# Weight parts made one step apart with four pairs of buffers, expert sums accumulated in token order, and a shorter index lookup in the routing

## The chip, the cores and the metric

The kernel runs on one core of a Trainium2 chip, as one program with one launch. The metric is the device time of that launch in microseconds (us). The median of three runs of the kernel before is 1644.19 us (1643.83 to 1645.55).

The engines are named as the profile names them: PE multiplies matrices, and PEld is its weight load. DVE, ACT and POOL work on vectors. SP issues the transfers (DMA) of the weights.

## The reference

Two transformer blocks on 256 tokens of 1024 numbers, all in fp32. What matters here:

```python
# block 1: mLSTM and window attention -> w_out; cross attention -> w_xo; then the experts:
qh = (xb @ w_pq).reshape(T, P_HEADS, 2, P_KEY_DIM)             # 8 heads, two halves
s1, s2 = scores of both halves against 128 sub keys each
v1, i1 = lax.top_k(s1, 16);  v2, i2 = lax.top_k(s2, 16)
cand_s = v1[..., :, None] + v2[..., None, :]                   # 16 x 16 candidates
cand_i = i1[..., :, None] * 128 + i2[..., None, :]
top_s, pos = lax.top_k(cand_s, 16)
eidx = take_along_axis(cand_i, pos);  g = softmax(top_s)
a = gelu(einsum('thkd,td->thk', expert_down[eidx], xb))
out = einsum('thk,thkd->td', g * a, expert_up[eidx])           # 16384 experts
# block 2: rms norms of h (g_final, norm_mix), then w_in_2 (GLA and MoBA), w_branch, w_out_2, MLP, gate
```

## The kernel before

**Activations lie transposed.** `hT`, `XH` and `XL` hold 8 blocks of 128 features by 256 tokens. An fp32 product is made of three matmuls on rounded parts: the activation is `XH + XL`, the weight is `hi + lo`, and `mm3` (lines 322 to 325) adds hi·XH, hi·XL and lo·XH. One *unit* takes one weight tile of 128 x 1024. In the transposed form (`unit_T`, line 327) that is 24 matmuls of 256 columns, with the weight as the loaded operand. In the token form (`unit_N`, line 349; lines 362 to 364) it is 12 matmuls of 512 columns, with the activation loaded and the weight streaming.

**All weights come as one stream** (`Stream`, line 86), in the order of `ORDER`. `load` issues the DMA of a raw tile on SP's queue. `cut_upto` makes the two parts right after one another: `hi` is a cast, on ACT (lines 119 to 122), and `lo = raw - hi` is on DVE or POOL (line 123). `PLAN` says where: "AV" is ACT then DVE, "AG" is ACT then POOL, from the named tile on. `take` hands out one pair, after it has cut up to two tiles ahead. There are four raw tiles and three pairs of parts.

**Side work is threaded through the units** (`Chains`, line 137). Norms, attention and routing are generators. Each finished unit calls `tick`, which runs one step of every live chain, and `yield n` waits n units (`PAUSES` adds to it). A chain's step is thus queued on each engine behind the unit's evacuation. While the chain named by `gate` lives, finished units keep their PSUM bank, and five banks exist.

**The places that matter.** After the eight units `xo` of the cross attention, each evacuation adds to `hT` and makes `XH`, `XL` and a sum of squares (`add_and_prep`, line 376). Sixteen units `pq` follow, with the norm's chain `norm_chain` (line 308). Then come 128 units `down` (one per 128 experts). While these run, `routing` (line 861) does the top-k work on DVE for each of the two token blocks: sixteen `top16` of 128 scores, two in a step, then eight steps with the 16 x 16 sums and a `top16` of 256, then the softmax. The index lookup (lines 889 to 903) runs twice for each block: it compares 2048 numbers with 0 to 15, multiplies by the index, and reduces, in fp32. PE transposes what came out. After that `gating` scatters the gates, four tokens in each unit.

The stage UP (lines 970 to 995) multiplies the 128 expert tiles by their coefficients: `coef` makes both parts of 256 coefficients per tile, and `up` uses the weight as the loaded operand, 24 matmuls of 256 columns in a tile. Its sums come out transposed and are added to `hT` bank by bank. Block 2 then begins with the units `bk` of `SECOND`, which are in token form.

## Time and profile before

| | |
|---|---|
| median of the runs | 1644.19 us |
| the profiled execution | 1648.56 us, of which the span is 1646.8 us |
| PE busy | 1572.9 us, 96% of the span |
| DVE, ACT, POOL busy | 73%, 49%, 24% of the span |
| granted PE clock, mean | 0.981 of 2.4 GHz |
| `down` with the routing beside it | 300 to 505 us |
| `down` with the gating beside it | 505 to 750 us |
| UP | 753 to 1121 us |

A matmul of 256 columns is recorded as some 0.28 us long, but the next one starts 0.12 us after it: they overlap, so a full PE shows as busy and the pace has to be read from the starts. What PE waits for is told by the idle time before an instruction and by what ended it.

### The profile page before, as it was taken

What the parts mean: (1) busy time and instruction counts of PE and PEld (TensorE: products, weight loads), DVE (VectorE), ACT (ScalarE), POOL (GpSimd) and SP (SyncE); (2) the same over time, 40 slices, a digit from 0 to 9 for tenths busy, and PEclk for the clock granted to TensorE, in tenths of its full rate; (3) what the DMA queues carried; (4) which work ended last, traced back from release to release, by engine and by line L of the source; (5) the groups of instructions that cost most, each with busy time, mean ns of one, the idle gap of its engine ahead of it and who ended that gap; (6) DMA issues with size and microseconds to landing.
All of it is one profiled execution on the core that took longest, in us unless ns stands there. A gap on an engine that the chain in (4) does not pass through costs nothing.

```text
span 1646.8 us, 30594 instructions
## 1 busy us (share of the span) xinstructions
PE 1572.9 (96%) x12338; PEld 1515.7 (92%) x12338; DVE 1207.7 (73%) x2073; ACT 798.9 (49%) x1336; POOL 392.0 (24%) x223
## 2 busy tenths in 40 slices
PE   9889989989879999999999999999899999899998
PEld 8788989988879999999999999998698899899998
DVE  6967653788978899976666666668885566777556
ACT  7555443543334555544444444445464643444444
POOL 3210004435530000003444444421030100087000
PEclk9999999999989999999999999999999999999999
DMA  7334444334334444445665555665445345455653
GB/s 263 103 103 156 139 145 154 131 131 162 128 123 158 156 154 154 154 168 178 183 185 184 180 180 184 186 186 166 152 143 164 119 163 179 159 175 190 201 180 128
DMA packets 75726, 265.52 MB, mean 161 GB/s; under 512 B 8368, under 2 KB 11952, under 8 KB 75584
## 3 DMA queue, kind: packets, MB, share of 16 engines
q1 hardware_dynamic: 74848, 262.31, 48.7%
q8 instruction: 96, 1.57, 0.4%
q10 hardware_dynamic: 736, 1.27, 0.2%
q14 instruction: 46, 0.38, 0.1%
HBM read 262.49 MB, written 1.05 MB: 160 GB/s over the span
## 4 chain that ended last, share of the span: by engine, by line
PE 63%; DVE 6%; ACT 1%; issue 1%; POOL 0%; DVEq 0%; POOLq 0%; ACTq 0%
PE mm L323 11%; PE mm L325 11%; PE mm L324 10%; PE at L987 6%; PE at L988 6%; PE at L989 6%; DVE lo L123 2%; PE mm L989 2%; PE mm L988 2%; PE mm L987 2%; PE at L941 2%; PE mm L363 2%; PE mm L362 2%; PE mm L364 2%; ACT hi L122 1%
## 5 line engine op out<-in xcount | busy, mean ns | idle before, releaser
L122 ACT CAST hi<-raw 128x1024 fp32r<-128x1024 f32 (+1 forms) x495 | 515.6, 1044 | 301.0 <-issue 104.9
L123 DVE TENSOR_TENSOR lo<-raw,hi 128x1024 fp32r<-128x1024 f32 (+1 forms) x376 | 469.9, 1252 | 167.1 <-ACT hi L122 164.0
L123 POOL TENSOR_TENSOR lo<-raw,hi 128x1024 fp32r<-128x1024 f32 x119 | 296.2, 2489 | 843.5 <-ACT hi L122 708.4
L325 PE MATMUL mm<-XH,lo 128*128 128x256 f32 x1608 | 464.3, 289 | 32.2 <-DVE lo L123 31.5
L323 PE MATMUL mm<-XH,hi 128*128 128x256 f32 x1608 | 470.9, 293 | 4.8 <-DVE hT L378 4.3
L324 PE MATMUL mm<-XL,hi 128*128 128x256 f32 x1608 | 461.7, 287 | 0.0
L325 PEld LDWEIGHTS mm<-XH,lo 128*128 128x128 f32 x1608 | 315.6, 196 | 35.9 <-DVE lo L123 34.8
L323 PEld LDWEIGHTS mm<-XH,hi 128*128 128x128 f32 x1608 | 315.9, 196 | 6.6 <-issue 5.1
L324 PEld LDWEIGHTS mm<-XL,hi 128*128 128x128 f32 x1608 | 315.9, 196 | 0.2
L975 DVE SCALAR_TENSOR_TENSOR ring<-cb,ring 128x256 fp32r<-128x256 f32 x128 | 173.0, 1353 | 94.1 <-ACT ring L974 94.1
L987 PE MATMUL at<-ring,hi 128*128 128x256 f32 x768 | 217.4, 283 | 1.0 <-DVE cb L961 1.0
L988 PE MATMUL at<-ring,hi 128*128 128x256 f32 x768 | 217.4, 283 | 0.0
L989 PE MATMUL at<-ring,lo 128*128 128x256 f32 x768 | 217.4, 283 | 0.0
L987 PEld LDWEIGHTS at<-ring,hi 128*128 128x128 f32 x768 | 147.4, 192 | 1.2 <-ACT ring L974 1.2
L988 PEld LDWEIGHTS at<-ring,hi 128*128 128x128 f32 x768 | 147.4, 192 | 0.1
L989 PEld LDWEIGHTS at<-ring,lo 128*128 128x128 f32 x768 | 147.5, 192 | 0.0
L958 ACT ACTIVATE cb<-mm 128x256 f32<-128x256 f32 (+32 forms) x117 | 38.2, 326 | 171.7 <-PE mm L325 171.7
L363 PE MATMUL mm<-lo,XH 128*128 128x512 f32 (+1 forms) x208 | 82.0, 394 | 4.8 <-DVE lo L123 4.7
L362 PE MATMUL mm<-hi,XH 128*128 128x512 f32 (+1 forms) x208 | 84.1, 404 | 1.0 <-ACT kn L1336 1.0
L364 PE MATMUL mm<-hi,XL 128*128 128x512 f32 (+1 forms) x208 | 81.6, 392 | 0.8 <-DVE XL L411 0.8
L325 PE MATMUL mm<-MH,lo 128*128 128x256 f32 x256 | 72.5, 283 | 2.0 <-POOL lo L123 1.2
L988 PE MATMUL mm<-ring,hi 128*128 128x256 f32 x256 | 72.5, 283 | 0.0
(460 smaller groups left out, 2932.0 us busy)
## 6 DMA issues: line engine op xcount, KB each, us to landing
raw<-in_wst SPq DMA_DIRECT2D x237, 512.0 KB, 3.3
raw<-in_dwn SPq DMA_DIRECT2D x128, 512.0 KB, 3.3
raw<-in_upw SPq DMA_DIRECT2D x128, 512.0 KB, 4.1
hT<-in_xT SPq DMA_DIRECT2D x4, 256.0 KB, 5.4
memt<-in_memT SPq DMA_DIRECT2D x1, 1024.0 KB, 6.0
out<-hT SPq DMA_DIRECT2D x7, 128.0 KB, 1.7
rowt<-in_rows ACTq DMA_DIRECT2D x1, 640.0 KB, 6.0
raw<-in_wst SPq DMA_DIRECT2D x2, 256.0 KB, 3.9
```

What stands on the lines that cost most here:

```text
L122: self.nc.scalar.copy(hi[:, o], raw[:, o])
L123: (self.nc.vector if second == "V" else self.nc.gpsimd).tensor_tensor(lo[:, o], raw[:, o], hi[:, o], op=OP.subtract)
L323: T.matmul(ps, lhsT=wh, rhs=xh, start=start, stop=False)
L324: T.matmul(ps, lhsT=wh, rhs=xl, start=False, stop=False)
L325: T.matmul(ps, lhsT=wl, rhs=xh, start=False, stop=stop)
L362: T.matmul(pss[tb], lhsT=xh, rhs=h, start=kd == 0, stop=False)
L363: T.matmul(pss[tb], lhsT=xh, rhs=l, start=False, stop=False)
L364: T.matmul(pss[tb], lhsT=xl, rhs=h, start=False, stop=kd == 7)
L975: V.scalar_tensor_tensor(lo, cb[:, j], 1.0 / GATE, hi, op0=OP.mult, op1=OP.subtract)
L987: T.matmul(o, lhsT=wh, rhs=ch, start=j == 0 and n % 2 == 0, stop=False)
L988: T.matmul(o, lhsT=wh, rhs=cl, start=False, stop=False)
L989: T.matmul(o, lhsT=wl, rhs=ch, start=False, stop=j == 127 and n % 2 == 1)
```

## The change

1. **The second part is made one step behind the first.** `cut_upto` first makes the `lo` of tiles whose `hi` was cut a step earlier, then the new `hi`. `take` cuts one tile further ahead (4 in place of 3), so at a unit `hi` stands three tiles ahead and `lo` two, as it did. Four pairs of parts and five raw tiles are kept.
2. **`PLAN`.** POOL makes the second parts of tiles xo2 to down19 and down28 to down44 (59 tiles; before, two in three of pq2 to down51). DVE makes those of down20 to down27 and of down45 to down127.
3. **UP in token form.** The coefficients are the loaded operand and 512 columns of the weight stream: 12 matmuls in a tile, into four PSUM banks. At the end the sums are copied to SBUF (two copies on ACT, two on DVE), turned by 16 transposes on PE, and only then added to `hT`; the second half of this is a chain that starts in the first tick of `bk`.
4. **The lookup** works on fp16, with a shape in which neighbouring numbers lie in pairs: 2048 compared, 2048 multiplied, and four additions that halve the 16 rows (1024, 512, 256 and 128) in place of the reduction. Each lookup step waits five units in place of four.
5. **Norms.** `norm_chain` waits two units before its last matmuls in place of one (three for the memory's; the first norm keeps one). `along` and `gla` wait one unit longer.
6. The coefficients of UP share their buffers with the gating's tiles.

```diff
+PLAN = {"mv0": ("AV",), "xo2": ("AG",), "down20": ("AV",), "down28": ("AG",), "down45": ("AV",),
+        "upw0": ("AV", "AG"), "upw122": ("AV",), "up3": ("AV", "AG"), "up31": ("AV",)}
...
-    def cut_upto(self, upto):
+    def cut_upto(self, upto, lag=1):
+        self.second_upto(upto - lag)
         while self.cut < min(upto, len(self.order)):
...
+    def second_upto(self, upto):
+        while self.second < min(upto, self.cut):
+            c = self.second
+            hi, eng = self.parts[c]
+            lo = self.split.tile([128, 1024], FR, tag="lo", name="lo")
+            raw = self.raws.pop(c)
+            for o in self.halves(c):
+                (self.nc.vector if eng == "V" else self.nc.gpsimd).tensor_tensor(lo[:, o], raw[:, o], hi[:, o],
+                                                                                op=OP.subtract)
...
-    ws = Stream(nc, rawp, splitp, order, 4, 3)
+    ws = Stream(nc, rawp, splitp, order, 4, 4)
...
-    def norm_chain(pool, tag, work, nat, dst, total=None, gap=1):
+    def norm_chain(pool, tag, work, nat, dst, total=None, gap=2):
...
+                    V.tensor_tensor(hit.rearrange("p k (c s) -> p k c s", s=2),
+                                    pf.rearrange("p (c s) -> p c s", s=2)[:, None].to_broadcast([128, 16, 64, 2]),
+                                    iota2[:, 0:16, None, :].to_broadcast([128, 16, 64, 2]), op=OP.is_equal)
+                    h5 = hit.rearrange("p k (h c s) -> p k h c s", h=8, s=2)
+                    V.tensor_tensor(h5, h5, two[:, :, :, None, :].to_broadcast([128, 16, 8, 8, 2]), op=OP.mult)
+                    for n in (8, 4, 2):
+                        V.tensor_tensor(hit[:, 0:n], hit[:, 0:n], hit[:, n:2 * n], op=OP.add)
+                    V.tensor_tensor(ee, hit[:, 0], hit[:, 1], op=OP.add)
+                    yield 5
...
+        def up(j, w, tb, g):
+            ch, cl = (c[:, tb * 128:tb * 128 + 128] for c in coefs[j])
+            wh, wl = (x[:, g * 512:g * 512 + 512] for x in w)
+            o = sums[g][tb]
+            T.matmul(o, lhsT=ch, rhs=wh, start=j == 0, stop=False)
+            T.matmul(o, lhsT=ch, rhs=wl, start=False, stop=False)
+            T.matmul(o, lhsT=cl, rhs=wh, start=False, stop=j == 127)
...
+            A.copy(nat2[:, 0, g * 512:g * 512 + 512], sums[g][0])
+            V.tensor_copy(nat2[:, 1, g * 512:g * 512 + 512], sums[g][1])
+        half(0)
```

Where this moves instructions, three places show it. First DVE's queue at the units `xo`, before: `hT` is the sum, `XL` the activation's second part, `acc` the squares' sum.

```order
L123 TENSOR_TENSOR lo<-raw,hi 128x1024
L378 TENSOR_TENSOR hT<-mm,hT 128x256
L289 SCALAR_TENSOR_TENSOR XL<-hT,colt,XH 128x256
L299 TENSOR_TENSOR acc<-acc,sq 128x256
L123 TENSOR_TENSOR lo<-raw,hi 128x1024
```

Each unit has one second part of a weight in this queue. The same place of the changed kernel, where the second part of the weight has gone to POOL's queue:

```order
L390 TENSOR_TENSOR hT<-mm,hT 128x256
L301 SCALAR_TENSOR_TENSOR XL<-hT,colt,XH 128x256
L311 TENSOR_TENSOR acc<-acc,sq 128x256
L390 TENSOR_TENSOR hT<-mm,hT 128x256
```

So nothing of the weight's stands between one unit's sum and the next.

Second, DVE's queue at the first lookup of a token block, before (`cb` holds all of the routing's buffers).

```order
L886 TENSOR_SCALAR gT<-at 128x128
L887 SCALAR_TENSOR_TENSOR gT<-at,gT 128x128
L891 TENSOR_SCALAR cb<-cb 128x128
L894 CAST cb<-cb 128x128
L895 TENSOR_TENSOR cb<-cb,iota 128x2048
L898 TENSOR_TENSOR cb<-cb 128x2048
L899 TENSOR_REDUCE cb<-cb 128x128
L123 TENSOR_TENSOR lo<-raw,hi 128x1024
L903 CAST eT<-at 128x128
```

The three operations on 2048 numbers (lines 895 to 899) are those that the change replaces. The same lookup changed:

```order
L908 CAST cb<-cb 128x256
L910 TENSOR_TENSOR cb<-cb,iota_93 128x2048
L914 TENSOR_TENSOR cb<-cb 128x2048
L916 TENSOR_TENSOR cb<-cb 128x1024
L916 TENSOR_TENSOR cb<-cb 128x512
L916 TENSOR_TENSOR cb<-cb 128x256
L917 TENSOR_TENSOR cb<-cb 128x128
L135 TENSOR_TENSOR lo<-raw,hi 128x1024 x5
L921 CAST eT<-at 128x128
```

Seven operations stand in place of three, and behind them five second parts of weights in place of one, since all of this stretch is DVE's own.

Third, DVE's queue at the end of UP, changed.

```order
L1059 COPY cb<-mm 128x512 x2
L1047 TENSOR_TENSOR hT<-at,hT 128x512
L1051 SCALAR_TENSOR_TENSOR XL<-hT,gfm,XH 128x256 x2
L1047 TENSOR_TENSOR hT<-at,hT 128x512
L1051 SCALAR_TENSOR_TENSOR XL<-hT,gfm,XH 128x256 x2
L135 TENSOR_TENSOR lo<-raw,hi 128x1024 x2
L1047 TENSOR_TENSOR hT<-at,hT 128x512
```

Two copies of the sums stand ahead of the additions, and the second parts of the tiles bk1 and bk2 between the two halves. Before, the additions to `hT` read the sums' banks themselves, and no transposes stood between.

## Rows read from the trace of the kernel before

**Rows 1.** The head of the profile's page.

```profile
span 1646.8 us, 30594 instructions
```

**Rows 2.** The view of windows: a stretch, its length, then the busy time (and instructions) of PE, PEld, DVE, ACT and POOL, the granted clock, the DMA share and GB/s.

```profile
300.00:505.00 205.00, 173.35 (x1316) 170.38 (x1315) 176.24 (x463) 79.53 (x118) 89.56 (x33) 0.92 0.39 137
...
750.00:1124.00 374.00, 372.99 (x3097) 372.32 (x3097) 256.22 (x206) 179.30 (x268) 144.18 (x60) 1.00 0.59 182
...
235.00:246.00 11.00, 6.69 (x38) 6.51 (x37) 4.74 (x8) 3.50 (x6) 2.37 (x1) 0.69 0.44 148
```

**Rows 3.** UP on PE: one of its lines (the first of three matmuls, with its first and last start), and two rows of the timeline, 24 matmuls apart (start, length).

```profile
L987 PE MATMUL at<-ring,hi x768: 281/283/355, 752.7 to 1119.7; 128*128 128x256 f32 x192
...
800.04 0.28 PE L987 MATMUL at<-ring,hi 128*128 128x256 f32 x1
...
802.92 0.28 PE L987 MATMUL at<-ring,hi 128*128 128x256 f32 x1
```

**Rows 4.** Matmuls of 512 columns in the timeline: in block 2, two rows 12 matmuls apart, and in the cross attention, two rows 3 apart.

```profile
1244.62 0.39 PE L362 MATMUL mm<-hi,XH 128*128 128x512 f32 x1
...
1247.34 0.39 PE L362 MATMUL mm<-hi,XH 128*128 128x512 f32 x1
...
204.93 0.39 PE L362 MATMUL mm<-hi,memh 128*128 128x512 f32 x1
...
205.63 0.39 PE L362 MATMUL mm<-hi,memh 128*128 128x512 f32 x1
```

**Rows 5.** The routing's stretch, 300 to 505 us: PE's matmuls of one line (there are three such lines), and what PE waited for (us in total, times, the longest).

```profile
L323 PE MATMUL mm<-XH,hi 128*128 128x256 f32 x432 | 128.4, 297 | 0.0
...
PE mm L325 <- DVE lo L123: 29.3, 12, 6.6
PE at L902 <- DVE cb L899: 1.7, 1, 1.7
```

**Rows 6.** DVE's groups in the same stretch: count, busy us, mean ns of one; the last row is a fp16 operation of the gating.

```profile
L123 DVE TENSOR_TENSOR lo<-raw,hi 128x1024 fp32r<-128x1024 f32 x20 | 31.6, 1589 | 11.7 <-ACT hi L122 11.7
L898 DVE TENSOR_TENSOR cb<-cb 128x2048 f32<-128x2048 f32 x4 | 15.4, 3856 | 0.1
L872 DVE TENSOR_TENSOR cb<-cb 128x256 f32<-128x256 f32 x16 | 15.1, 946 | 0.0
L895 DVE TENSOR_TENSOR cb<-cb,iota 128x2048 f32<-128x2048 f32 x4 | 11.3, 2826 | 0.1
...
L899 DVE TENSOR_REDUCE cb<-cb 128x128 f32<-128x2048 f32 x4 | 9.1, 2286 | 0.1
...
L918 DVE TENSOR_TENSOR hots<-eT,iota 128x1024 f16<-128x1024 f16 x1 | 0.7, 681 | 0.0
```

**Rows 7.** DVE's timeline in the routing: the starts of two `top16` of 128 scores that follow one another, and of two steps with the 16 x 16 sums.

```profile
403.22 0.29 DVE L855 MAX8 cb<-cb 128x8 f32<-128x128 f32 x1
...
404.80 0.28 DVE L855 MAX8 cb<-cb 128x8 f32<-128x128 f32 x1
...
352.10 0.41 DVE L872 TENSOR_TENSOR cb<-cb 128x256 f32<-128x256 f32 x1
...
354.80 0.41 DVE L872 TENSOR_TENSOR cb<-cb 128x256 f32<-128x256 f32 x1
```

**Rows 8.** POOL's timeline in the routing: second parts alone, beside DVE's, and beside lines 895 and 898.

```profile
423.88 2.38 POOL L123 TENSOR_TENSOR lo<-raw,hi 128x1024 fp32r<-128x1024 f32 x1 [6.52 <-ACT hi L122]
426.76 2.84 POOL L123 TENSOR_TENSOR lo<-raw,hi 128x1024 fp32r<-128x1024 f32 x1 [0.50 <-ACT hi L122]
...
472.93 4.13 POOL L123 TENSOR_TENSOR lo<-raw,hi 128x1024 fp32r<-128x1024 f32 x1 [0.23 <-ACT hi L122]
```

**Rows 9.** The timeline of two evacuations in the units `xo`, and the first matmul of `pq`; in brackets the idle time before an instruction and what ended it.

```profile
229.35 0.42 DVE L378 TENSOR_TENSOR hT<-mm,hT 128x256 f32<-128x256 f32 x1
...
230.53 1.03 ACT L122 CAST hi<-raw 128x1024 fp32r<-128x1024 f32 x1
...
231.59 1.23 DVE L123 TENSOR_TENSOR lo<-raw,hi 128x1024 fp32r<-128x1024 f32 x1 [0.42 <-ACT hi L122]
...
232.74 0.42 DVE L378 TENSOR_TENSOR hT<-mm,hT 128x256 f32<-128x256 f32 x1
...
240.06 0.55 PE L323 MATMUL mm<-XH,hi 128*128 128x256 f32 x1 [4.31 <-DVE hT L378]
```

**Rows 10.** What PE waited for elsewhere: at 130 to 300 us, at 1124 to 1200 us (block 2 begins) and at 1395 to 1446 us (`wo2` and the first `up`).

```profile
PE at L305 <- DVE cb L318: 1.6, 1, 1.6
...
PE mm L363 <- DVE lo L123: 2.9, 4, 1.1
...
PE mm L325 <- DVE lo L123: 2.8, 5, 0.8
PE at L305 <- DVE dg L318: 1.6, 1, 1.6
PE mm L325 <- POOL lo L123: 1.2, 1, 1.2
```

**Rows 11.** What the new end of UP is made of, from where it stands now: ACT's copies of 512 sums, four transposes of 128 x 128 on PE (the next matmul starts at 1309.91), and the additions to `hT`.

```profile
L851 ACT COPY cb<-at 128x512 f32<-128x512 f32 x8 | 4.7, 596 | 0.3 <-PE at L837 0.3
...
1309.56 0.60 PE L1328 MATMUL at<-ident,og 128*128 128x128 f32 x4
...
L1013 DVE TENSOR_TENSOR hT<-at,hT x3: 683/690/692, 1118.1 to 1120.3; 128x512 f32<-128x512 f32 x3
```

More of the change, by code (lines that the diff above doesn't have):

```diff
@@ L91, in __init__ @@
         self.order, self.depth, self.ahead = order, depth, ahead
[L92 removed]
+        self.loaded = self.cut = self.second = self.taken = 0
         self.raws, self.parts = {}, {}
@@ L122, in cut_upto @@
                     self.nc.scalar.copy(hi[:, o], raw[:, o])
-                (self.nc.vector if second == "V" else self.nc.gpsimd).tensor_tensor(lo[:, o], raw[:, o], hi[:, o],
-                                                                                   op=OP.subtract)
+            self.parts[c] = (hi, second)
+            self.cut += 1
+            self.second_upto(upto - lag)
+    def second_upto(self, upto):
[7 more added lines that the diff above has]
+                                                                                op=OP.subtract)
             self.parts[c] = (hi, lo)
-            self.cut += 1
+            self.second += 1
     def take(self, name, kept=0):
@@ L423, in first_norm @@
             yield 2
-            yield from norm_chain(psA, "at", wk, rx, Rb)
+            yield from norm_chain(psA, "at", wk, rx, Rb, gap=1)
         ch.start("norm", first_norm(), "norm0")
@@ L449, in mem_chain @@
             yield 1
-            yield from norm_chain(psA, "at", wk, rm, Rm, total=accm, gap=2)
+            yield from norm_chain(psA, "at", wk, rm, Rm, total=accm, gap=3)
         ch.start("mem", mem_chain())
@@ L970, in block_kernel @@
         coefs = {}
+        ring = {}
         def coef(j):
-            hi, lo = (big.tile([128, 256], FR, tag="ring", name="ring", bufs=8) for _ in range(2))
+            if j % 3 == 0:
+                ring[0] = big.tile([128, 3, 2, 256], FR, tag="hots", name="ring", bufs=2)
+            hi, lo = ring[0][:, j % 3, 0], ring[0][:, j % 3, 1]
             A.activation(hi, cb[:, j], AF.Copy, scale=1.0 / GATE)
@@ L979, in block_kernel @@
         psB = ctx.enter_context(tc.tile_pool(name="psB", bufs=4, space=PSUM))
-        sums = [bank(psB, "at") for i in range(3)] + [bank(psB, "mm")]
+        sums = [[bank(psB, "mm") for tb in range(2)] for g in range(2)]
+        nat2 = flat[:, 4096:6144].rearrange("p (a d) -> p a d", a=2)
         coef(0)
         coef(1)
-        def up(j, w, n):
-            o = sums[n // 2][:, (n % 2) * 256:(n % 2) * 256 + 256]
-            wh, wl = (x[:, n * 128:n * 128 + 128] for x in w)
-            ch, cl = coefs[j]
-            T.matmul(o, lhsT=wh, rhs=ch, start=j == 0 and n % 2 == 0, stop=False)
-            T.matmul(o, lhsT=wh, rhs=cl, start=False, stop=False)
-            T.matmul(o, lhsT=wl, rhs=ch, start=False, stop=j == 127 and n % 2 == 1)
+        def up(j, w, tb, g):
[5 more added lines that the diff above has]
+            T.matmul(o, lhsT=cl, rhs=wh, start=False, stop=j == 127)
         for j in range(126):
@@ L1006, in square, with half, second_half @@
             A.activation(sq1[:, k2], hT[:, k2], AF.Square)
-        for i in range(4):
-            for n in (2 * i, 2 * i + 1):
-                for j in range(2):
-                    up(126 + j, last[j], n)
-            k2 = slice(2 * i, 2 * i + 2)
-            V.tensor_tensor(hT[:, k2], sums[i].rearrange("p (a t) -> p a t", a=2), hT[:, k2], op=OP.add)
-            if i == 3:
-                ws.cut_upto(ws.taken + 2)
-                square(2)
-            for n in (2 * i, 2 * i + 1):
-                A.activation(XH[:, n], hT[:, n], AF.Copy, scale=gfm[:, n:n + 1])
-            for n in (2 * i - 2, 2 * i - 1) if i < 3 else (4, 5, 6, 7):
-                if n >= 0:
+        def half(g):
+            turned = {}
+            for i in (2 * g, 2 * g + 1):
+                turned[i] = bank(psB, "at")
+                for k in range(2):
+                    for tb in range(2):
+                        o = (2 * i + k) * 128
+                        T.transpose(turned[i][:, k * 256 + tb * 128:k * 256 + tb * 128 + 128], nat2[:, tb, o:o + 128],
+                                    ident)
+            for i in (2 * g, 2 * g + 1):
+                k2 = slice(2 * i, 2 * i + 2)
+                V.tensor_tensor(hT[:, k2], turned[i].rearrange("p (a t) -> p a t", a=2), hT[:, k2], op=OP.add)
+                for n in (2 * i, 2 * i + 1):
+                    A.activation(XH[:, n], hT[:, n], AF.Copy, scale=gfm[:, n:n + 1])
+                for n in (2 * i, 2 * i + 1):
                     V.scalar_tensor_tensor(XL[:, n], hT[:, n], gfm[:, n:n + 1], XH[:, n], op0=OP.mult,
                                            op1=OP.subtract)
-            if i != 2:
-                square(i)
+        for g in range(2):
+            for tb in range(2):
+                for j in range(2):
+                    up(126 + j, last[j], tb, g)
+            A.copy(nat2[:, 0, g * 512:g * 512 + 512], sums[g][0])
+            V.tensor_copy(nat2[:, 1, g * 512:g * 512 + 512], sums[g][1])
+        half(0)
+        ws.cut_upto(ws.taken + 2)
+        square(0)
+        square(1)
+        def second_half():
+            half(1)
+            yield 1
+            square(2)
+            square(3)
+        ch.start("half", second_half())
         ws.cut_upto(ws.taken + 3)
```

45 lines of the change are left out of this document (19 added, 26 removed).

## The prediction

> **What bounds the kernel now.** The head of the page gives the span, 1646.8 us [rows 1]; PE's busy share of 96% says little, since its matmuls overlap. So I read PE's pace first, by the starts in the timeline, and then everywhere the waits that end in a PE instruction. The windows show two kinds of stage. In UP, 24 matmuls of a tile take from 800.04 to 802.92, 2.88 us or 120 ns each [rows 3], and PE is busy for 372.99 of 374 us at full clock [rows 2]: there only fewer or faster matmuls help. While the routing runs beside `down`, PE's three lines have 432 matmuls each [rows 5]: 3 x 432 x 0.12 = 155.5 us, with some 2 us for the small ones 157.5, in a window of 205 us [rows 2]. So 47 us are lost. Waits for `lo` on DVE are 29.3 us, one for a lookup's result is 1.7 [rows 5], and the rest is the clock, granted at 0.92 [rows 2]: the full 2.4 GHz falls to its half, 1.2 GHz, behind some of these waits. DVE is busy for 176 us in that window. It is the bound there, and PE stands behind it.
>
> **UP in token form.** It removes 128 x 24 = 3072 matmuls of 256 columns, 3072 x 0.120 = 368.6 us [rows 3], and adds 1536 of 512 columns. This form runs elsewhere in the kernel: in block 2, 12 matmuls start from 1244.62 to 1247.34, 226.7 ns each; in the cross attention 3 take 0.70 us, 233 ns [rows 4]. I take the first, the longer undisturbed stretch: 348.2 us, or **-20.4**. The other end is 1536 x 0.233 = 357.9, -10.7. ACT has a cast of 1.03 us [rows 9] and a small coefficient cast in each tile of 2.72 us, POOL 2.4 us in every second one [rows 8], DVE 1.23 us in the others [rows 9] and the coefficients, some of them behind POOL: all fit.
>
> **The end of UP.** Now PE turns the sums: four transposes take from 1309.56 to 1309.91 [rows 11], so 16 take 1.4 us. Ahead of `bk0` stand a copy of 512 sums (0.6 on DVE, by ACT's 596 ns) and the addition (0.69) [rows 11], then XH on ACT (some 0.5): 1.8 us, of which the first half's transposes cover 0.7, so PE waits some 1.2. DVE then has both additions, four XL and the two weights' parts of bk1 and bk2 before the second half. I count its queue against PE's 2.72 us for a unit: bk1, bk2 and bk3 each get something late, 0.5, 0.5 and 1.2 us. Sum **+4.8**. Nothing below the transposes' 1.4 is possible; at worst all four waits double, +8.2.
>
> **The routing.** POOL now makes the second parts of 20 of the first 20 and 17 of the next 25 tiles, so DVE's 20 at 1.59 us [rows 6] shrink to the lookups' stretches, where POOL is idle. What remains on DVE, for each token block: 16 `top16` of 1.575 us (403.22 to 404.80 for one), 3.15 in a step; eight steps of 2.70 (352.10 to 354.80) [rows 7]; softmax, some 2.3; two lookups. A lookup of fp16 is, at 0.681 us for 1024 numbers [rows 6], 1.36 + 1.36 + 0.68 + 0.34 + 0.25 + 0.2 = 4.2 us with 1.2 for the small ones ahead of it: 5.4. Before it was 3 x 2.29 free, but 898 took 3.86 and 895 2.83 in the mean, since each waited for POOL [rows 6]. If fp16 saves nothing, two operations stay at 2.29 and a lookup costs 7.3.
>
> All this is 2 x (25.2 + 21.6 + 2.3) + 4 x 5.4 = 120 us, with 22 second parts of 1.23 (27 us) 147, for 56 units of 2.88 = 161 us. So PE should become the bound, except where DVE falls behind locally. The steps with `top16` exceed a unit by 0.27; the sums of line 872 take 0.41 free and 0.95 in the mean, as they wait for POOL [rows 6], so those steps may go at POOL's pace of one in 2.88 us. In the second block this makes 25.2 + 7 x 2.88 + up to 1.5 = 46.9 us before the first DVE-made part (tile 45) is begun; it ends at 48.1, and PE wants it 16 units = 46.1 us after the block's begin: 1.8 late (with its first matmuls), then 1.1 and 0.7 for the next two, 3.6 us in all. Behind each lookup the next tile's part must be ready 5.76 us after the lookup could start, and 5.4 + 0.4 (transpose) + 1.23 is 7.0: some 1.1 us late, four times, once with 1 us of lag more: 5.4. With two or three falls of the clock at some 1 us each I leave 12 of the 47 us: **-35**. Bounds: nothing left but the clock, -44; fp16 without gain (4 x 1.9 more) and POOL's waits on every step, -20.
>
> Four more units pass before the gating starts, at unit 57; it needs 64 of the remaining 71, so no tail is added.
>
> **The units `xo` and the norm behind them.** An evacuation comes every 3.39 us (229.35 to 232.74), because the sum, XH, the cast (1.03) and the second part (1.23) follow one another on two engines [rows 9]; PE needs 2.8 and pays at the end, 4.31 us [rows 9] and a clock of 0.69 in 235 to 246, worth 3.4 us [rows 2]. With the cast a step ahead and the second part on POOL, DVE has some 1.4 us of work and a wait for XH; XL may wait for POOL, 2.4 at most, which still fits one unit. The norm's wait of 1.6 [rows 10] meets 2.88 us more. Of 9.3 I leave 2.3: **-7**; POOL in the way of XL and of the norm's small operations would leave 7, nothing would leave 0.
>
> **Elsewhere.** The other norm's 1.6 and the waits for second parts, 2.9, 2.8 and 1.2 [rows 10], are 8.5 us. A part that no longer waits for its own cast takes a gap out of DVE's queue, but where DVE itself is late (block 2's begin) it changes nothing: **-5**, between -8.5 and +2 (the shifted chains, the start's waits).
>
> **Sum.** -20.4 + 4.8 - 35 - 7 - 5 = -62.6. The profiled execution took 1648.56 us, so 1586.0. The runs' median, 1644.19, lies 4.4 below it, and I forecast 1581.6.
>
> **The rivals.** *DVE stays the bound of the routing.* For: it stands at 176 of 205 us now, and each step exceeds a unit; against: the sum of 147 in 161. It is so if the lookup costs 7.3 us or more and every line 872 waits. Then 15 of the 35 us come, and the time is 1602.
>
> *UP gains nothing.* This is so if the time over the columns (120 against 256 / 2.4 = 107 ns) grows with the columns and isn't one for each matmul: 512 would take 240, and 1536 x 0.240 = 368.6. Then the time is 1602 also. Against: both rows of 512 columns lie below 240 [rows 4]. The Trainium skill (TensorE: Matmul & The Clock Gate, Back-to-back issue gap) puts a matmul's gap at N / 2.4 + 2.5 ns, 109 and 216, by which, as an estimate, UP would gain 3.9 us alone and the time would be 1598. Neither figure is what the rows have.
>
> *POOL becomes the bound, and the kernel is slower.* POOL takes 2.38 us alone, 2.84 beside DVE's second part, and 4.13 beside lines 895 and 898 [rows 8]: the two wait for each other. A unit leaves it 2.88 - 2.40 = 0.48 us. If DVE's operations take it so often that it needs 4.13 each, its 59 tiles cost 59 x 1.25 = 74 us and the routing's 35 are gone: 1581.6 + 109 = 1690. It decides from a mean of 3.35 us on (59 x 0.47 = 27.6 us, what is then left). Against: `top16` and reductions run at one length beside POOL, the sums of line 872 hold it for 0.41, and the lookups stand where POOL has nothing to do. The Trainium skill (SBUF — State Buffer, Who interferes with whom) says that of two such operations the first to start has the port for its whole length and the other blocks. By that rule each meeting costs the second one the first one's rest, and the trace agrees: 0.95 for 0.41.
>
> **How the numbers follow.** Forecast 0.75; DVE still the bound 0.13; no gain in UP 0.08; POOL the bound 0.04. The low end is the forecast with nothing left in `xo` and little in the routing, some -17 more: 1565. The high end takes in the two middle rivals at 1602: 1605. A change of under 0.2% (3.3 us) cannot be told from none. Faster by more: all but the last rival and a little, 0.95; within 0.01; slower 0.04.
>
> **What would show it.** In the profile after: matmuls of 512 columns in UP starting every 227 ns and PE without a wait there; the wait for DVE's `lo` in the routing's stretch under 10 us (29.3 before) and the clock there over 0.96; the wait ahead of `pq` under 2 us; a new wait of 1 to 2 us and 16 transposes behind UP; POOL's mean under 2.6 us. The prediction is wrong if DVE's fp16 lookups cost as much as the fp32 ones, if POOL's mean is over 2.88, or if block 2's begin waits for more than 8 us in addition.

## The result and the profile after

The changed kernel takes 1566.68 us, the median of four runs (1563.34 to 1568.26). The kernel before, on the same chip, takes 1644.01 us (1643.33 to 1645.55, four runs). The ratio is 0.9526, its 95% interval 0.9509 to 0.9543. The profiled execution has a span of 1565.1 us, against 1646.8 [rows 1], so 81.7 us less. Some 4 us of these are the profiled execution of before, which lay that much over its median; the medians differ by 77.3.

The page of the kernel after: the span, and the groups of second parts on POOL and DVE (count, busy us, mean ns, then the idle time ahead and what ended it). The last row is DVE's group on the page of the kernel before.

```profile
span 1565.1 us, 27519 instructions
...
L135 POOL TENSOR_TENSOR lo<-raw,hi 128x1024 fp32r<-128x1024 f32 x134 | 325.1, 2427 | 737.8 <-ACT hi L123 735.3
L135 DVE TENSOR_TENSOR lo<-raw,hi 128x1024 fp32r<-128x1024 f32 (+1 forms) x361 | 447.8, 1250 | 24.2 <-ACT hi L123 24.0
...
L123 DVE TENSOR_TENSOR lo<-raw,hi 128x1024 fp32r<-128x1024 f32 (+1 forms) x376 | 469.9, 1252 | 167.1 <-ACT hi L122 164.0
```

POOL's mean is 2.43 us, and DVE stands for only 24 us ahead of its second parts, where it stood for 167.

The windows of the kernel after, the same stretch as in [rows 2] (now with some 46 us of the gating's part in it) and UP:

```profile
300.00:505.00 205.00, 198.04 (x1685) 195.94 (x1684) 168.87 (x463) 99.19 (x163) 71.38 (x30) 1.00 0.52 167
697.80:1046.20 348.40, 348.37 (x1536) 288.21 (x1537) 248.79 (x196) 174.26 (x256) 141.81 (x60) 1.00 0.61 193
```

The routing has the full clock now, 1.00 against 0.92. UP is full, as before, but shorter.

What PE waited for in the kernel after (us in total, times, the longest): in the routing, at 150 to 280 us, and behind UP. The rows of before are those of [rows 5] and [rows 10].

```profile
PE mm L337 <- DVE lo L135: 6.9, 7, 2.4
...
PE at L317 <- DVE cb L330: 2.8, 1, 2.8
PE mm L335 <- DVE hT L390: 0.6, 1, 0.6
...
PE mm L375 <- DVE lo L135: 2.6, 4, 0.8
...
PE mm L374 <- ACT XH L1049: 1.0, 1, 1.0
```

The waits in the routing fell from 29.3 to 6.9 us. The norm's wait beside `pq` (line 317) grew from 1.6 [rows 10] to 2.8. The wait ahead of `pq` (line 335) is 0.6, where it was 4.31 [rows 9]. The last row is the new wait behind UP.

The timeline of the kernel after: UP, its end, the norm beside `pq` on DVE and POOL, a second lookup with the parts behind it, and the first and the last operation of a lookup with no part of POOL's beside it.

```profile
800.19 0.39 PE L1013 MATMUL mm<-hi,ring 128*128 128x512 f32 x1
...
802.91 0.39 PE L1013 MATMUL mm<-hi,ring 128*128 128x512 f32 x1
...
1046.35 1.03 PE L1043 MATMUL at<-ident,cb 128*128 128x128 f32 x8
1048.44 0.50 PE L374 MATMUL mm<-hi,XH 128*128 128x512 f32 x1 [1.05 <-ACT XH L1049]
...
232.26 2.23 DVE L282 TENSOR_SCALAR nwi<-nwm 128x2 int32<-128x2 int32 x1
234.40 0.15 DVE L283 TENSOR_SCALAR nwh<-nwm 128x2 f32<-128x2 f32 x1
234.53 2.33 DVE L284 TENSOR_SCALAR rn<-nwi 128x2 int32<-128x2 int32 x1
236.89 2.40 DVE L294 SCALAR_TENSOR_TENSOR nww<-rn,nwh 128x1 f32<-128x1 f32 x2
...
232.05 7.09 POOL L135 TENSOR_TENSOR lo<-raw,hi 128x1024 fp32r<-128x1024 f32 x3 [2.07 <-PE at L326]
...
358.99 3.54 DVE L916 TENSOR_TENSOR cb<-cb 128x1024 f16<-128x1024 f16 x3
362.57 0.29 DVE L917 TENSOR_TENSOR cb<-cb 128x128 f32<-128x128 f16 x1
362.77 4.55 DVE L135 TENSOR_TENSOR lo<-raw,hi 128x1024 fp32r<-128x1024 f32 x2
...
428.82 0.22 DVE L903 TENSOR_SCALAR cb<-cb 128x128 uint32<-128x128 uint32 x1
...
433.45 0.29 DVE L917 TENSOR_TENSOR cb<-cb 128x128 f32<-128x128 f16 x1
```

In UP 12 matmuls start in 2.72 us, 226.7 ns each. At its end eight transposes take 1 us and PE waits 1.05 more. Beside `pq` three rows of DVE on two numbers or one per partition last 2.2 to 2.4 us (the row of 2.40 is two operations), and each ends within 0.2 us of the end of one of POOL's three parts.

Since both kernels run the same units in the same order, the start of each unit's first matmul in the timelines tells where the time went:

| stage | starts before, us | starts after, us | gain in the stage, us |
|---|---|---|---|
| start to `xv` | 0 | 0 | 10.6 |
| `xo` | 212.8 | 202.2 | 3.8 |
| `pq` | 240.1 | 225.7 | 1.6 |
| `down` | 301.1 | 285.1 | 38.9 |
| UP | 752.7 | 697.8 | 18.2 |
| `bk` | 1121.5 | 1048.4 | -1.1 |
| `bq` to the end | 1146.0 | 1074.0 | 9.7 |
| end | 1646.8 | 1565.1 | sum 81.7 |

Of the last 9.7, 6.2 lie in `wa`, `wo2` and the first `up`, 1.5 in `bq`, 1.5 in `gv`, 0.6 in `ga`.

### The profile page after: what moved, and what is told of

Its sections match the earlier page's. It is cut to its first block, busy times and chain, and to the rows that moved or that the text cites. A ratio compares the mean times of both kernels' runs of the same rounds, so it can differ in the third digit from the quotient of the medians.

```text
span 1565.1 us, 27519 instructions
## 1 busy us (share of the span) xinstructions
PE 1530.9 (98%) x10818; PEld 1419.4 (91%) x10818; DVE 1145.3 (73%) x2070; ACT 800.3 (51%) x1338; POOL 425.7 (27%) x238
## 3 DMA queue, kind: packets, MB, share of 16 engines
HBM read 262.49 MB, written 1.05 MB: 168 GB/s over the span
## 4 chain that ended last, share of the span: by engine, by line
PE 83%; DVE 13%; issue 1%; ACT 1%; DMA 1%; POOL 0%; SPq 0%; DVEq 0%; ACTq 0%; POOLq 0%
PE mm L335 16%; PE mm L337 16%; PE mm L336 16%; PE mm L1015 7%; PE mm L1013 7%; PE mm L1014 7%; DVE lo L135 3%; PE mm L376 2%; PE mm L374 2%; PE mm L375 2%; PE at L959 2%; DVE cb L872 1%; DVE cb L869 1%; DVE scr L1280 1%; DVE cb L871 1%
## 5 line engine op out<-in xcount | busy, mean ns | idle before, releaser
L135 POOL TENSOR_TENSOR lo<-raw,hi 128x1024 fp32r<-128x1024 f32 x134 | 325.1, 2427 | 737.8 <-ACT hi L123 735.3
L135 DVE TENSOR_TENSOR lo<-raw,hi 128x1024 fp32r<-128x1024 f32 (+1 forms) x361 | 447.8, 1250 | 24.2 <-ACT hi L123 24.0
L337 PE MATMUL mm<-XH,lo 128*128 128x256 f32 x1608 | 455.9, 283 | 7.5 <-DVE lo L135 7.5
L337 PEld LDWEIGHTS mm<-XH,lo 128*128 128x128 f32 x1608 | 308.5, 192 | 9.1 <-DVE lo L135 9.1
L335 PEld LDWEIGHTS mm<-XH,hi 128*128 128x128 f32 x1608 | 308.6, 192 | 2.0 <-issue 1.5
L1013 PE MATMUL mm<-hi,ring 128*128 128x512 f32 x512 | 199.3, 389 | 1.0 <-DVE cb L979 1.0
L1015 PE MATMUL mm<-hi,ring 128*128 128x512 f32 x512 | 199.3, 389 | 0.0
L1014 PE MATMUL mm<-lo,ring 128*128 128x512 f32 x512 | 199.2, 389 | 0.0
L1013 PEld LDWEIGHTS mm<-hi,ring 128*128 128x128 f32 x512 | 96.1, 188 | 21.0 <-ACT ring L997 1.2
L1015 PEld LDWEIGHTS mm<-hi,ring 128*128 128x128 f32 x512 | 96.1, 188 | 20.2 <-DVE ring L998 0.4
L1014 PEld LDWEIGHTS mm<-lo,ring 128*128 128x128 f32 x512 | 96.1, 188 | 20.1
L335 PE MATMUL mm<-u,hi 128*128 128x256 f32 x256 | 71.7, 280 | 0.0
```

The lines of the kernel that those rows point to most:

```text
L135: (self.nc.vector if eng == "V" else self.nc.gpsimd).tensor_tensor(lo[:, o], raw[:, o], hi[:, o], op=OP.subtract)
L335: T.matmul(ps, lhsT=wh, rhs=xh, start=start, stop=False)
L337: T.matmul(ps, lhsT=wl, rhs=xh, start=False, stop=stop)
L1013: T.matmul(o, lhsT=ch, rhs=wh, start=j == 0, stop=False)
L1014: T.matmul(o, lhsT=ch, rhs=wl, start=False, stop=False)
L1015: T.matmul(o, lhsT=cl, rhs=wh, start=False, stop=j == 127)
```

## The experiments

The theory was that the step apart is worth more than the forecast gave it, since a second part that waits for its cast holds up all that stands behind it in DVE's queue. Its rivals were the plan, the pauses and the deeper buffers. The table has each kernel's time and ratio to the kernel before (run beside it; the ratio is what compares), and by how many us each stage of its profiled execution is longer than in the changed kernel. The changed kernel's own ratio is 0.9526 (0.9509 to 0.9543). The intervals of e6, e7, e8, e10 and e12 overlap it, so what these gain or lose is read from the stages alone, of one execution each. Where kernels do not differ, the stage up to `xo` scatters by some 1 us, and `gv` by 1.3.

| kernel | us | ratio, 95% | to `xo` | `xo` | `pq` | `down` | UP | `bk` | rest |
|---|---|---|---|---|---|---|---|---|---|
| e1_no_lag | 1583.97 | 0.9619 (0.9591-0.9647) | 8.9 | 0 | -3.6 | 0.2 | -0.2 | 5.2 | 6.8 |
| e5_lag_alone | 1612.12 | 0.9789 (0.9768-0.9811) | 1.5 | 0.1 | 1.7 | 25.9 | 18.7 | -2.8 | 1.0 |
| e9_deeper_no_lag | 1573.07 | 0.9568 (0.9542-0.9594) | 8.1 | 0 | -1.5 | -4.8 | -0.2 | 0 | 4.9 |
| e3_old_plan | 1590.25 | 0.9654 (0.9633-0.9675) | 0.5 | 0.1 | 2.4 | 24.2 | 0 | 0 | -1.5 |
| e4_fp32_lookup | 1579.93 | 0.9597 (0.9571-0.9623) | -1.2 | 0 | 0 | 14.3 | 0 | 0 | -0.3 |
| e8_pool_lookups | 1569.65 | 0.9544 (0.9518-0.9569) | -0.1 | 0 | -1.5 | 3.0 | 0 | 0 | 0.4 |
| e2_old_up | 1583.80 | 0.9632 (0.9606-0.9658) | 0.8 | 0 | -0.1 | 0 | 18.7 | -1.9 | -0.1 |
| e7_norm2_later | 1568.35 | 0.9540 (0.9514-0.9566) | -0.8 | 0 | 1.6 | 1.0 | 0 | 0 | -0.1 |
| e6_old_pauses | 1572.26 | 0.9556 (0.9531-0.9580) | 2.4 | 0 | 2.0 | 1.1 | 0 | 0.1 | 1.1 |
| e12_norm2_dve | 1562.74 | 0.9496 (0.9469-0.9524) | 0 | 0 | -4.5 | 1.1 | 0 | 0 | 0.1 |
| e10_plan_moved | 1563.01 | 0.9505 (0.9476-0.9534) | 0.3 | 0 | -0.1 | -2.6 | 0 | 0 | -1.4 |
| e11_improved | 1554.72 | 0.9448 (0.9423-0.9473) | 0.5 | 0 | -4.5 | -6.2 | 0 | 0 | 0.1 |

### The step apart: e1_no_lag, e5_lag_alone, e9_deeper_no_lag

e1_no_lag undoes it and keeps the buffers (the last two numbers of `Stream` are how many raw tiles are loaded ahead and how many tiles are cut ahead):

```diff
-    def cut_upto(self, upto, lag=1):
+    def cut_upto(self, upto, lag=0):
...
-    ws = Stream(nc, rawp, splitp, order, 4, 4)
+    ws = Stream(nc, rawp, splitp, order, 5, 3)
...
-        ws.cut_upto(ws.taken + 2)
+        ws.cut_upto(ws.taken + 1)
...
-        ws.cut_upto(ws.taken + 3)
+        ws.cut_upto(ws.taken + 2)
```

> The changed kernel, but each second part stands right behind its own first part again, at the place in the queues where the second part stands now; buffers, loads and everything else stay. Theory (the step apart is worth more than I took, because a second part that waits for its cast blocks whatever of DVE is queued behind it, in every stage): DVE's idle time ahead of second parts rises from 24 us to over 120, the 10.6 us that the changed kernel gains before the units xo fall to under 4, and the time is 1580 to 1595 us. Rival (these gains come from the longer pauses of the chains and from POOL's share, not from the step): within 5 us of 1566.7, with over 8 us of the gain before xo kept.

Measured: 1583.97 us, as the theory has it. The span is 17.3 us longer, 8.9 of the 10.6 us before `xo` are gone, and DVE's idle time ahead of its second parts is 123.3 us on the page, 24.2 in the changed kernel. What DVE (the first row) and PE waited for in e1_no_lag at 60 to 200 and 60 to 215 us:

```profile
DVE lo L135 <- ACT hi L123: 17.0, 18, 3.3
...
PE mm L375 <- DVE lo L135: 3.2, 4, 1.6
PE at L656 <- ACT pA L669: 1.8, 1, 1.8
PE at L667 <- ACT pA L669: 1.7, 2, 1.1
PE at L335 <- ACT qx L698: 1.5, 2, 0.8
PE at L558 <- DVE oW L660: 1.0, 1, 1.0
```

The first row is not there at all in the changed kernel. In e1_no_lag DVE stands 18 times for the cast that its part reads, 17 us in all. PE's waits for `lo` are 3.2 us against 2.4 in the changed kernel; what is new is named for the attention's `pA`, `qx` and `oW`. So little of this loss carries the name `lo`. The theory holds there and in the rest (6.8), and `bk` loses 5.2. In `down` the step is worth nothing beside the new plan (0.2), and in `pq` it costs 3.6.

e5_lag_alone puts the step alone into the kernel before; its `Stream` is that of the changed kernel:

```diff
-    rawp = ctx.enter_context(tc.tile_pool(name="rawp", bufs=4))
-    splitp = ctx.enter_context(tc.tile_pool(name="splitp", bufs=3))
+    rawp = ctx.enter_context(tc.tile_pool(name="rawp", bufs=5))
+    splitp = ctx.enter_context(tc.tile_pool(name="splitp", bufs=4))
...
-    ws = Stream(nc, rawp, splitp, order, 4, 3)
+    ws = Stream(nc, rawp, splitp, order, 4, 4)
```

> The kernel before with the first part of the change alone: second parts one step behind, four pairs, five raw tiles (UP's coefficients share the gating's buffers, to make the room); plan, UP, lookup and pauses as before. Theory (step apart): 20 to 32 us faster than before, 1612 to 1624, of which 8 to 11 us before the units xo and some 6 behind gb; the waits for DVE's second parts in the routing remain over 12 us of the 31.5. Rival (the step is worth little without the plan): under 8 us faster, 1636 to 1644.

Measured: 2.1% faster than before (the interval reaches from 1.9 to 2.3%), 35 us, over the theory's 32. Before `xo` it is within 1.5 us of the changed kernel, so the step, with the buffers that it needs, makes that gain alone; the buffers without it, in e1_no_lag, do not. It makes the gain in the units `xo` alone as well (0.1 from the changed kernel), with POOL in no part of it. Of the 38.9 us in `down` it brings 13. PE's wait for DVE's second parts there is still 21.0 us:

```profile
PE mm L339 <- DVE lo L135: 21.0, 10, 5.3
```

e9_deeper_no_lag gives depth in place of the step:

```diff
-    def cut_upto(self, upto, lag=1):
+    def cut_upto(self, upto, lag=0):
```

> The changed kernel without the step apart, but with both parts made three tiles ahead of their use (in the changed kernel the second stands two ahead), from the same four pairs and five raw tiles. It tells why the step apart gains outside the routing. Theory (DVE stands still for its own cast, and what is queued behind it, the attention's and the norms' small operations, comes late): DVE's idle time ahead of second parts is again over 120 us, at least 7 of the 8.9 us before xo that e1_no_lag lost stay lost, and the time is 1574 to 1584. Rival (the second parts themselves were late, and any deeper queue mends it): the time is within 5 us of 1566.7.

Measured: 1573.07, just under the theory's range and over the rival's. DVE's idle time ahead of its second parts is 147.1 us on the page. What DVE waited for at 60 to 200 us in e9_deeper_no_lag:

```profile
DVE lo L135 <- ACT hi L123: 16.5, 18, 3.3
```

DVE stands as long as in e1_no_lag, and 8.1 us before `xo` stay lost, while PE waits for no second part there at all: it is the standing, not late parts. In `bk` it is the other way: the depth alone mends what e1_no_lag lost (0 against 5.2), so there the parts themselves were late. In `down` depth gains 4.8 us over the changed kernel. Neither of the two theories covers the whole kernel. A kernel with the step ahead of `xo` and the depth in `down` was not run.

### Plan and lookup: e3_old_plan, e4_fp32_lookup, e8_pool_lookups

```diff
-PLAN = {"mv0": ("AV",), "xo2": ("AG",), "down20": ("AV",), "down28": ("AG",), "down45": ("AV",),
-        "upw0": ("AV", "AG"), "upw122": ("AV",), "up3": ("AV", "AG"), "up31": ("AV",)}
+PLAN = {"mv0": ("AV",), "pq2": ("AG", "AG", "AV"), "down52": ("AV",), "upw0": ("AV", "AG"), "upw122": ("AV",),
+        "up3": ("AV", "AG"), "up31": ("AV",)}
```

> The changed kernel with the plan of before (POOL makes two in three second parts of pq2 to down51). DVE's sum in the routing is then the same 147 us, since it makes 22 parts either way; only their places differ. Theory (the plan is worth what the places give): DVE falls behind by some 9 us in each token block ahead of the lookups (2.2 from the steps over a unit, 5 parts of 1.23), of which half comes back, and xo loses some 4; 12 to 22 us slower than the changed kernel, 1579 to 1589. Rival (the sum alone decides, the step apart hides the places): within 5 us of 1566.7.

Measured: 21 us slower than the changed kernel by the ratios, at the theory's upper end. The profiled execution, the slowest of the four, has 24.2 us more in `down`, and none in `xo`, where the theory had 4. What PE waited for in e3_old_plan's routing:

```profile
PE mm L337 <- DVE lo L135: 20.4, 10, 4.5
```

That is 13.5 us more than in the changed kernel; the granted clock at 288 to 500 us is 0.94 against 1.00, which can be the other part (as an estimate, 0.06 x 212 = 12.7 us). Of down0 to down55 DVE makes 21 parts here and 19 in the changed kernel, so most of the loss is due to the places: the four lookups, three of them beside POOL's parts again, take 37.3 us of DVE in place of 21.7.

e4_fp32_lookup has the old three operations again:

```diff
...
+                    V.tensor_tensor(cand.rearrange("p h a b -> p (h a) b"),
+                                    pf[:, :, None].to_broadcast([128, 128, 16]),
+                                    iota[:, None].to_broadcast([128, 128, 16]), op=OP.is_equal)
+                    V.tensor_tensor(cand, cand, ff[:, :, half, None, :].to_broadcast([128, 8, 16, 16]), op=OP.mult)
+                    V.tensor_reduce(ee, cand.rearrange("p h a b -> p (h a) b"), axis=AX.X, op=OP.add)
...
```

> The changed kernel with the fp32 lookup of before (three operations on 2048 numbers), all else as changed. Theory (the four lookups are on the path): each takes 3 x 2.29 = 6.9 us in place of 4.2, and PE waits for most of the 2.7 more, 1575 to 1578. Rival (the units beside a lookup hide it): under 3 us, 1567 to 1570.

DVE's groups in e4_fp32_lookup's routing, and what PE waited for there:

```profile
L912 DVE TENSOR_TENSOR cb<-cb 128x2048 f32<-128x2048 f32 x4 | 9.2, 2292 | 0.1
L909 DVE TENSOR_TENSOR cb<-cb,iota 128x2048 f32<-128x2048 f32 x4 | 9.2, 2292 | 0.1
L913 DVE TENSOR_REDUCE cb<-cb 128x128 f32<-128x2048 f32 x4 | 9.1, 2286 | 0.1
...
PE mm L339 <- DVE lo L135: 16.9, 6, 5.0
```

Measured: 14.3 us more in `down`, over the theory's 8 to 11; by the ratios the whole kernel loses 12. The four lookups hold DVE for 29.8 us in place of 21.7, and two casts of the indices for 1.8 more. PE's waits for DVE's second parts rise from 6.9 to 16.9 us, so about the whole of it reaches PE. The clock of 0.98 over 216 us can make the rest (4.3, an estimate). The multiplication (line 912, line 898 before) takes 2.29 where it took 3.86 [rows 6]: in three of the four lookups no part of POOL's runs beside it, and in the fourth it had begun first and POOL's part took 3.2 us.

e8_pool_lookups gives POOL the stretch of the lookups:

```diff
-PLAN = {"mv0": ("AV",), "xo2": ("AG",), "down20": ("AV",), "down28": ("AG",), "down45": ("AV",),
+PLAN = {"mv0": ("AV",), "xo2": ("AG",), "down45": ("AV",),
```

> The changed kernel with POOL making all second parts up to down44, those beside the first block's two lookups too (down20 to down27). Theory (POOL's parts and the lookup's fp16 operations take turns, each operation of DVE behind a whole part of POOL, 2.4 us): PE no longer waits at down21 and down26 (3.5 us), but a lookup's six operations take 10 to 17 us in place of 4.2, the second block's steps begin some 5 us late, and PE pays that at down45; 1566 to 1570. Rival (POOL becomes the bound, as the prediction's last rival has it): POOL's mean over 2.88 us in that stretch and PE waiting for POOL's second parts, slower than the changed kernel by over 5 us. Third (the meetings are cheap): 3 to 5 us faster.

The timeline of DVE and POOL in e8_pool_lookups at the first lookup, and one of PE's waits in its routing:

```profile
339.21 1.74 DVE L903 TENSOR_SCALAR cb<-cb 128x128 uint32<-128x128 uint32 x1
340.99 2.31 DVE L906 CAST cb<-cb 128x128 f16<-128x128 uint32 x1
...
346.91 3.31 DVE L914 TENSOR_TENSOR cb<-cb 128x2048 f16<-128x2048 f16 x1
350.25 7.62 DVE L916 TENSOR_TENSOR cb<-cb 128x1024 f16<-128x1024 f16 x3
...
345.85 11.88 POOL L135 TENSOR_TENSOR lo<-raw,hi 128x1024 fp32r<-128x1024 f32 x4 [0.27 <-ACT hi L123]
...
PE at L920 <- DVE cb L917: 5.3, 1, 5.3
```

Measured: this lookup takes 19.0 us (339.21 to 358.19, the end of line 917), where one alone takes 4.9. Seven of POOL's parts run beside it; the last four take 11.88, 2.97 each in place of 2.40. So DVE pays 14 us for these meetings and POOL 2.3. POOL did not become the bound: its mean is 2.47 us at 300 to 413 us, and PE waits for none of its parts. The time fits the theory, but PE paid at another place, for the transpose of the lookup's result (5.3 us), whose five units of pause no longer cover it.

### UP: e2_old_up

```diff
+        sums = [bank(psB, "at") for i in range(3)] + [bank(psB, "mm")]
...
+            T.matmul(o, lhsT=wh, rhs=ch, start=j == 0 and n % 2 == 0, stop=False)
+            T.matmul(o, lhsT=wh, rhs=cl, start=False, stop=False)
+            T.matmul(o, lhsT=wl, rhs=ch, start=False, stop=j == 127 and n % 2 == 1)
```

> The changed kernel with UP and its end in the form of before (24 matmuls of 256 columns in a tile, sums transposed). Theory (the pace of a matmul is a fixed time over its columns, and nothing of UP's vector work is late): UP takes 20.4 us more, the end without copies and transposes about 3 less, so 16 to 18 us slower than the changed kernel, 1583 to 1585, and no unit outside UP and the first units bk differs by over 0.5 us. Rival (the token form gains by something else, such as fewer weight loads beside the vector work): the pace of the 256-column matmuls differs from 120 ns here.

Measured: UP is 18.7 us longer, `bk` 1.9 shorter, nothing else moves by over 0.8, which is the scatter of the first stage. The net gain of the token form is 16.8 us here, as the theory has it. 24 matmuls of 256 columns start in 2.88 us, 120 ns each, so the rival is out.

### The norm beside `pq`: e7_norm2_later, e6_old_pauses, e12_norm2_dve

```diff
-          ("gla", 1): 1, ("gla", 8): 1, ("gla_out", 2): 1}
+          ("gla", 1): 1, ("gla", 8): 1, ("gla_out", 2): 1, ("norm2", 1): 1}
```

> The changed kernel with one more unit of pause in the norm beside pq (three units in place of two). In the trace after, three of that norm's small operations on DVE take 2.2 to 2.4 us in place of 0.2 to 0.35, as they stand beside three second parts of POOL that follow one another, and PE waits for 2.9 us. Theory (one unit covers that wait, a fifth bank holds the unit kept): 2.3 to 3.3 us faster, 1563.5 to 1564.5. Rival (the units kept meanwhile are written out late, and PE waits for a bank instead): no change.

What PE waited for in e7_norm2_later at 215 to 285 us:

```profile
PE at L317 <- DVE cb L330: 2.1, 1, 2.1
PE mm L335 <- DVE cb L386: 0.9, 1, 0.9
```

Measured: no gain, `pq` 1.6 us longer, so my theory fell. POOL had four parts in a row beside the norm in place of three, which delayed the norm by one more part; PE's wait at line 317 was still 2.1 us. The second row is a wait for the kept units to be written out, as the rival has it, and takes 0.9. The two waits together are 3.0 us, 0.2 over the changed kernel's 2.8; the rest goes with the granted clock, 0.94 in this stage against 0.97.

```diff
-    def norm_chain(pool, tag, work, nat, dst, total=None, gap=2):
+    def norm_chain(pool, tag, work, nat, dst, total=None, gap=1):
...
-          ("along", 1): 3,
+          ("along", 1): 2,
...
-          ("gla", 1): 1, ("gla", 8): 1, ("gla_out", 2): 1}
+          ("gla", 8): 1, ("gla_out", 2): 1}
```

> The changed kernel with the chains' pauses of before (norms wait one unit, the memory's two, along and gla as before). Theory (beside pq a longer pause only lets another second part of POOL follow, as e7_norm2_later showed, so a shorter one costs nothing there; elsewhere the pauses are worth the 3.0 us that bq to gv gained and that e1_no_lag and e9_deeper_no_lag did not lose there): 2 to 5 us slower than the changed kernel, 1569 to 1572, with pq within 1.5 us. Rival (each pause covers its units): pq alone loses 2.9 more, 1573 or over.

Measured: 0.3% slower than the changed kernel by the ratios, whose intervals overlap; by the stages 6.7 us. `pq` loses 2.0, between the two expectations: two operations of DVE met a part of POOL's, not three, and PE's wait at line 317 is 3.6 in place of 2.8, so a shorter pause costs less than its 2.9. `bq` loses 1.5 as expected; the 1.5 of `gv` do not come from the pauses, and stay open with that stage's scatter.

e12_norm2_dve takes the parts away that the norm meets:

```diff
-PLAN = {"mv0": ("AV",), "xo2": ("AG",), "down20": ("AV",), "down28": ("AG",), "down45": ("AV",),
+PLAN = {"mv0": ("AV",), "xo2": ("AG",), "pq4": ("AV",), "pq7": ("AG",),
+        "down20": ("AV",), "down28": ("AG",), "down45": ("AV",),
```

> The changed kernel with the three second parts beside the norm of pq (pq4 to pq6) made by DVE, behind the norm's operations in its queue. Theory (those small operations are long because each stands behind one of POOL's parts): lines 282, 284 and 294 take 0.2 to 0.4 us again, PE's wait of 2.9 us ahead of line 317 goes, 2.5 to 4 us faster, 1563 to 1564. Rival (the operations are long for another reason, or the three parts come late on DVE): no change, and PE waits for pq4's second part instead.

The same operations in the timeline of e12_norm2_dve (its lines are one further down):

```profile
232.31 0.17 DVE L283 TENSOR_SCALAR nwi<-nwm 128x2 int32<-128x2 int32 x1
...
232.51 0.17 DVE L285 TENSOR_SCALAR rn<-nwi 128x2 int32<-128x2 int32 x1
232.71 0.35 DVE L295 SCALAR_TENSOR_TENSOR nww<-rn,nwh 128x1 f32<-128x1 f32 x2
```

Measured: they take 0.17 to 0.35 us for 2.2 to 2.4, PE's wait is gone, and `pq` is 4.5 us shorter: the wait's 2.8, and a granted clock of 1.00 where the changed kernel has 0.97. That the meetings with POOL made the wait is shown. `down` is 1.1 us longer behind it, as in e6 and e7. In all three the granted clock at 355 to 380 us is 0.93, behind a wait of 2.4 us for the part of down26; in the changed kernel it is 1.00 behind the same wait. Why it fell in the three and not there is open.

### Both mendings: e10_plan_moved, e11_improved

```diff
-PLAN = {"mv0": ("AV",), "xo2": ("AG",), "down20": ("AV",), "down28": ("AG",), "down45": ("AV",),
+PLAN = {"mv0": ("AV",), "xo2": ("AG",), "down20": ("AV",), "down26": ("AG",), "down27": ("AV",),
+        "down28": ("AG",), "down48": ("AV",), "down54": ("AG",), "down55": ("AV",),
```

> The changed kernel, with five second parts given from DVE to POOL: those of down26 and down54, behind a block's second lookup, and of down45 to down47, the first that DVE makes behind the top-k steps. In the changed kernel PE waits there for 2.6 and 0.6, and for 1.5, 1.0 and 0.1 us. Theory (DVE is late locally and POOL idle): 4 to 6 us faster than the changed kernel, 1561 to 1563. Rival (POOL's parts beside the lookup's fp16 operations make each other wait, as the 3.5 us of line 916 beside POOL in the trace after, 1.5 without): no faster, 1565 to 1569.

Measured: 2.6 us less in `down`. The waits behind the second block's steps (down45 and down46) went, as the theory has it, but the one at down26 moved to down27 (2.1 us), whose part DVE makes behind a lookup that POOL's parts made longer: the rival is right there.

```diff
-PLAN = {"mv0": ("AV",), "xo2": ("AG",), "down20": ("AV",), "down28": ("AG",), "down45": ("AV",),
+PLAN = {"mv0": ("AV",), "xo2": ("AG",), "pq4": ("AV",), "pq7": ("AG",),
+        "down20": ("AV",), "down21": ("AG",), "down22": ("AV",), "down26": ("AG",), "down48": ("AV",), "down49": ("AG",),
+        "down50": ("AV",), "down54": ("AG",), "down55": ("AV",),
```

> Both mendings together: pq4 to pq6 on DVE, and in the routing POOL makes the second parts of down21, of down26 to down47, of down49 and of down54 (in e10_plan_moved the wait of down26 only moved to down27, since DVE made that one behind a lookup that POOL had delayed). If the two theories hold, the waits for second parts in the routing fall from 6.9 to under 2 us and the norm's wait goes: 7 to 10 us faster than the changed kernel, 1557 to 1560. If POOL's parts beside the lookups cost what they give, 1561 to 1563.

What PE waited for in e11_improved's routing:

```profile
PE at L922 <- DVE cb L919: 1.7, 1, 1.7
PE mm L339 <- DVE lo L137: 0.2, 1, 0.2
```

Measured: 1554.72 us, 0.9448 of before; the interval ends at 0.9473, under that of the changed kernel. It beats both kernels; by the stages it gains 10 us on the changed one, the upper end of the 7 to 10 expected. The waits for second parts are 0.2 us. The 1.7 are the price of POOL's parts beside a lookup, as in e8_pool_lookups.

## Why the prediction was right, and where a term was off

The forecast was 1581.6 us, the median is 14.9 us below it, in the range but 2 us from its low end. That it is in the range is partly luck: the low end was worked out from what `xo` and the routing might give beyond their terms, and the excess came from elsewhere, where the prediction allowed for 3.5 us. By the stages, from the profiled executions:

| term | forecast, us | measured, us |
|---|---|---|
| UP's matmuls | -20.4 | -20.3 |
| the end of UP | +4.8 | +3.2 |
| the routing | -35 | -38.9 |
| `xo` and the norm behind it | -7 | -5.4 |
| elsewhere | -5 | -20.3 |

**UP.** The matmuls took 348.55 us (697.8 to 1046.35) against the 348.2 worked out from [rows 4]; the stage of before had 368.8. The rival of no gain is out: 226.7 ns, not 240. Nor is it the 216 ns that the Trainium skill (TensorE: Matmul & The Clock Gate, Back-to-back issue gap) has by its formula N / 2.4 + 2.5. That section gives the formula for an isolated matmul and says that it over-counts in a stream, a condition that the prediction does not take up; here the stream is slower than the formula. The measurement decides.

**The end of UP.** 2.1 us of it stand ahead of `bk0` (1.0 of transposes, 1.05 of wait, where I had 0.7 and 1.2), 1.1 in `bk`. That `bk` came off so lightly is due to the step: without it e1_no_lag loses 5.2 there, which only more depth, in e9_deeper_no_lag, wins back.

**The routing.** DVE stopped being the bound. The late parts came at the tiles that the prediction names: down45 and the next, and behind the four lookups (down21, down26, down49, down54), 6.9 us in all where I had 9.0. The clock didn't fall at all, for which I had left 3. Three of the four lookups met no part of POOL's and took 4.9 us (428.82 to 433.74 for one), the other took 7.0 (355.88 to 362.86), where I had 5.4. The gain is the plan's and the lookup's together: undoing one gives 24.2 back, the other 14.3, and the step alone brought 13, so the three aren't a sum. Some of the 38.9 can be chance: among the runs of the kernel before, the longer spans have the lower granted clock (1646.4 us at 0.980, 1639.7 at 0.988), the profiled one is a long one, and its clock fell most in the routing [rows 2].

**`xo` and the norm.** The units `xo` gave 3.8, but POOL wasn't needed for it: with the step alone (e5_lag_alone) or with POOL alone (e1_no_lag) they are as short. The norm's wait, which I let vanish in one more unit of pause, grew to 2.8. The prediction saw "POOL in the way of XL and of the norm's small operations" and put it at 7 left; 3.9 were left.

**Elsewhere** is the step that was mis-sized, by 15 us. The prediction had the mechanism ("a part that no longer waits for its own cast takes a gap out of DVE's queue") and then priced it by PE's waits from 130 us on, most of them named `lo` [rows 10]. The gap is paid under other names: DVE stood for its casts for 164 us in the kernel before, by its page. Most of that cost nothing, but whatever stood behind the second part, the attention's operations above all, came later, and PE's wait bears their names. e1_no_lag and e9_deeper_no_lag show it: 8 to 9 of the 10.6 us before `xo` hang on this. In the last stages (6.2) the step counts too, as e1_no_lag shows with 6.8; with more depth in its place 4.9 are still lost. The pauses made some 1.5 in `bq`: e5_lag_alone and e6_old_pauses, with the old ones, lose just that. The 1.5 in `gv`, and that the profiled execution of before was itself 4.4 us over its median, are no part of the change that a run here shows.

**POOL as the bound** didn't come. Its mean was 2.43 us, and 2.97 where the meetings are thickest (e8_pool_lookups), under the 3.35 from which that rival decides; DVE pays. The Trainium skill (SBUF — State Buffer, Who interferes with whom) lets the first to start keep the port for its whole length; the three rows of 2.2 to 2.4 us, which end with POOL's three parts, agree. The price falls on each operation that meets a part, however little it does, which my 4.13 us for POOL [rows 8], taken beside two long operations of DVE, hid.
